# First mixer: input blocks and token projection as whole fp32 products without splits; the compression product in four groups of 32 columns

## The chip, the cores and the metric

The kernel runs on one core of one Trainium2 chip. The metric is the device time of one execution in microseconds (us). The engines: PE is TensorE (matrix products), DVE is VectorE, ACT is ScalarE, POOL is GpSimd, SP is SyncE, which only issues transfers here.

## The reference

Two layers of a causal decoder for 256 tokens of width 1024. The change lies in the first mixer of layer 0 alone: an input projection shared by a convolution branch and a sparse-attention branch. Cut to what it computes:

```python
a = val * jax.nn.sigmoid(gate)                     # 512 channels each, from the input projection
y = lax.conv_general_dilated(a, conv_w[:, None, :], ...)     # 31 taps, per channel
y = silu(layernorm(y + conv_b))

def compress_blocks(src, pos, w1, w2):             # once for keys, once for values
    blk = src[:, idx] + pos[None, None, :, None, :]          # 15 blocks of 32 tokens, stride 16
    blk = blk.transpose(0, 3, 1, 2, 4).reshape(B, NSA_KV_HEADS, n_cmp, CMP_LEN * HEAD_DIM)
    return jax.nn.gelu(blk @ w1) @ w2              # 2 heads x 15 blocks, 2048 -> 256 -> 64
...
h = h + concat(y, attention) @ w_out
```

After it come, per layer, an expert mixer (PEER) that multiplies by all 16,384 experts' keys and values, and gates; they are not changed.

## The kernel before, in words

Everything is held transposed: `h` is 128 partitions x 8 slices (kt) x 256 tokens. The PEER products run from about 170 us to the end and the change does not touch them; the function `u_dense` they share is only given a width argument.

**Splits.** A product of the mixer in full precision is made of three passes at a rounded type (fp32r). `split` (L264, L265) makes the rounded part `hnH` of the normed input on ACT and the rest `hnL` on DVE. Each weight block `wx` (128 x 1024, 512 KB, 16 blocks of `in_win`, then 8 of `in_wout`) is split in the same way: `prep_h` (L184) makes `wH` on ACT and `prep_l` (L197) makes `wL` on DVE. `u_block` then issues for each of the 8 kt three matmuls (`mm3`, L225, L226, L227), 24 for one block of 128 x 256 outputs.

**Fetches.** Blocks are fetched on SP (L166) into a ring of three buffers; a buffer is free again once `wL` is made, so DVE sets when a fetch may start.

**Order.** The table `STEPS` (L46) says in which order the pieces of the mixer are written: first four channel pairs of the convolution (8 blocks, in the loop of L474), then the steps of the table. C, K and Q are input blocks (the last, Q3, is block 15); T1 and T3 are convolution taps on PE (L442, on diagonal matrices `dg` that ACT makes, L441); W1 and W0 are the token projection `in_token` (values and gates, weights `wt` of 128 x 8 x 280, split in step S at L545 and L546); s0 to s3 are scores (L640, L642, then P on ACT at L649); M0 and M1 are `compress`; p0, p1 are scores against compressed keys (L604); w0 to w3 weigh the values (L674, L684, L692); L is one stage of the normalisation of the convolution (L713, L726). The other convolution taps run one by one on DVE (L459), three behind most steps. A scheduler then orders the instructions within each engine. The sums of squares for the norm (ACT L282, PE L306) stand behind the first block, and everything that leaves PE is scaled by the norm `rs` afterwards.

**compress(c)** (L565): 16 fp32 matmuls with 30 columns of blocks as weights and 256 columns of `w1` as moving operand, into 30 partitions (L569); Gelu on ACT into `hid` (L572, with a table load before it); two transposes (L575); a copy `hT` (L578); the product with `w2` (L584 or L587).

Of the kernel before, what the change touches and what calls it, by code (L numbers as in the profile page):

```python
# [35 lines left out]
RINGS, ROWBUFS, AHEAD = (3, 10), 7, 8  # L36
# [9 lines left out]
STEPS = ("T1 Q1 C0 C1 K0 K1 B1 Q0 Q2 T3 B0 S W1 Q3 s0 M0 s1 W0 s2 p0 M1 w0 L w1 s3 p1 w2 L w3 L"  # L46
# [9 lines left out]
class Trunk:  # L56
# [72 lines left out]
    def plan(self):  # L129
# [22 lines left out]
        self.split_range(0, at["wq", 0] + 7)  # L152
# [90 lines left out]
    def u_dense(self, k, x):  # L243

        w = self.raw_block(k)
        out = self.bank()[:, :ND]
        for kt in range(KT):
            m = self.nc.tensor.matmul(out, w[:, kt * 128:kt * 128 + 128], x[:, kt, :ND],  # L248
                                      start=kt == 0, stop=kt == KT - 1)
        self.last_mm[k] = m  # L250
        self.raw_done(k)
        return out
# [145 lines left out]
    def mixer_even(self, st):  # L398
# [3 lines left out]
        base = self.at["in"]  # L402

# [70 lines left out]
        for c in range(4):  # L474
            pv = self.u_block(base + 2 * c)
# [4 lines left out]
            pg = self.u_block(base + 2 * c + 1)  # L480
# [19 lines left out]
        def in_kc(c):  # L500

            pk = self.u_block(next(nxt))
# [6 lines left out]
            blk.append((mp.tile([128, 16, 2, 15], F32, name=f"blk{c}"), E))  # L509
# [5 lines left out]
        def in_k(c):  # L515
            pk = self.u_block(next(nxt))
            for g in range(2):
                r = slice(g * 64, g * 64 + 64)
                nc.vector.tensor_tensor(out=kz[r, g, c], in0=pk[r], in1=self.rs[r], op=ALU.mult)

        def blocks(c):
            bt, E = blk[c]
            for g in range(2):
                v = E[g][:, 1:257].rearrange("p (n r) -> p r n", r=16)
                for hf in range(2):
                    pos = cpos[:, c, hf * 8:hf * 8 + 8, None].to_broadcast([128, 8, 15])
                    nc.vector.tensor_tensor(out=bt[:, hf * 8:hf * 8 + 8, g],
# [4 lines left out]
        def in_q(c):  # L532
            pq = self.u_block(next(nxt))
# [3 lines left out]
        wtH = mp.tile([128, KT, 280], F32R, name="wtH")  # L537
        wtL = mp.tile([128, KT, 280], F32R, name="wtL")
        vt = mp.tile([128, 2, 256], F32, name="vt")
        gt = mp.tile([128, 2, 24], F32, name="gt")  # L540

        def split_wt():
            for hf in range(2):
                s = slice(hf * 4, hf * 4 + 4)
                nc.scalar.activation(wtH[:, s], wt[:, s], AF.Copy)  # L545
                nc.vector.tensor_tensor(out=wtL[:, s], in0=wt[:, s], in1=wtH[:, s].bitcast(F32),  # L546
                                        op=ALU.subtract)

        def in_token(tt):
            pv = self.bank()[:, :280]  # L550
            s = slice(tt * 128, tt * 128 + 128)
            for kt in range(KT):
                self.mm3(pv, self.hnH[:, kt, s], self.hnL[:, kt, s], wtH[:, kt], wtL[:, kt],
                         kt == 0, kt == KT - 1)
# [10 lines left out]
        def compress(c):  # L565

            ph = self.bank()
            for lp in range(16):
                nc.tensor.matmul(ph[0:30, :256], blk[c][0][:, lp].rearrange("p g n -> p (g n)"),  # L569
                                 w1[c][:, lp], start=lp == 0, stop=lp == 15)  # L570
            hid = mp.tile([30, 256], F32, name="hid", bufs=1)
            nc.scalar.activation(hid, ph[0:30, :256], AF.Gelu_apprx_tanh)  # L572
            pt = self.bank()
            for m in range(2):
                nc.tensor.transpose(pt[:, m * 32:m * 32 + 30], hid[:, m * 128:m * 128 + 128],  # L575
                                    self.ident[0:30, 0:30])
# [246 lines left out]
    def peer_and_ple(self, l, st):  # L823
# [63 lines left out]
        for i in range(NB):  # L887
# [11 lines left out]
            ps = self.u_dense(base + i, hn)  # L899
# [553 lines left out]
```

## Time and profile before

| what | us |
|---|---|
| median of 3 runs (lowest, highest) | 1529.66 (1528.58, 1530.78) |
| the profiled execution's own time | 1531.44 |
| its span, first to last instruction | 1529.7 |
| PE busy in the span | 1499.5 (98%) |
| DVE, ACT, POOL busy | 1142.0, 684.7, 446.1 |
| the mixer: first matmul to the first product with `wout` | 5.56 to 128.82 |

A busy PE is one with a matmul under way; the granted clock tells separately how fast it ran (mean 0.993 of full). In the timeline, "start us" is the time from the span's start, and a row with xN is N instructions in a row as one. The duration of a matmul contains the time in which its results drain, so what a stream of them costs is read from the distance of their starts.

### The profile page before, as it was taken

The numbers are of one execution on the slowest core, as the hardware profiler recorded it, in microseconds if no ns is written. First come the engines' busy times: TensorE is split into PE (matmuls) and PEld (weight loads), VectorE is DVE, ScalarE is ACT, GpSimd is POOL, SyncE is SP. The second block draws the span as 40 slices with busy tenths as digits, with TensorE's granted clock in tenths as the row PEclk, the third lists the DMA queues.
The fourth block names the chain that finished last, engine by engine and source line by source line (L and its number), as shares of the span: only waits on it lengthen the run. The fifth ranks groups of instructions, "written<-read, shape, count | busy, mean of one in ns | idle before, by whom it ended". The sixth has DMA issues, their size and how long they took to land.

```text
span 1529.7 us, 30252 instructions
## 1 busy us (share of the span) xinstructions
PE 1499.5 (98%) x11882; PEld 1457.0 (95%) x11882; DVE 1142.0 (75%) x2752; ACT 684.7 (45%) x864; POOL 446.1 (29%) x406
## 2 busy tenths in 40 slices
PE   8999999999999999999998999999999999999997
PEld 8858999999999999999998999999999999999997
DVE  6997699988876888544448699987886788644446
ACT  6468321358863876000036321248872877000025
POOL 0000014343444333444300004343444333343400
PEclk9999999999999999999999999999999999999998
DMA  6603679999999999999985279999999999999980
GB/s 239 231 1 113 233 238 409 408 408 408 408 396 396 402 381 378 405 409 408 409 347 166 89 231 400 408 409 408 409 388 393 409 380 367 408 408 409 409 315 28
DMA packets 141245, 514.83 MB, mean 337 GB/s; under 512 B 15984, under 2 KB 16240, under 8 KB 140592
## 3 DMA queue, kind: packets, MB, share of 16 engines
q1 hardware_dynamic: 84384, 308.42, 52.6%
q0 software_dynamic: 55568, 202.66, 33.7%
q8 instruction: 94, 1.54, 0.4%
q10 hardware_dynamic: 1152, 1.82, 0.4%
q14 instruction: 47, 0.39, 0.1%
HBM read 511.53 MB, written 1.05 MB: 335 GB/s over the span
## 4 chain that ended last, share of the span: by engine, by line
PE 76%; DMA 12%; DVE 10%; ACT 1%; issue 1%; DVEq 0%; SPq 0%; ACTq 0%
PE bank_a L1015 28%; PE bank_a L248 26%; DMA wx<-in_v 9%; PE bank_g L1246 5%; PE bank_a L225 3%; PE bank_a L226 3%; PE bank_a L227 3%; DMA wx<-in_u 3%; DVE row L1341 2%; PE bank_a L569 1%; DVE rt_tmp L1033 1%; PE bank_a L640 1%; DVE yc L459 1%; PE bank_r L306 1%; DVE wL L197 1%
## 5 line engine op out<-in xcount | busy, mean ns | idle before, releaser
L1015 PE MATMUL bank_a<-z,wx 128*128 128x160 f32 x4096 | 574.6, 301 | 3.9 <-DMA wx<-in_v 1.0
L248 PE MATMUL bank_a<-hn,wx 128*128 128x160 f32 x4096 | 569.8, 300 | 2.1 <-DVE rt_gs L1204 1.2
L1015 PEld LDWEIGHTS bank_a<-z,wx 128*128 128x128 f32 x4096 | 559.3, 190 | 11.1 <-DMA wx<-in_v 11.0
L248 PEld LDWEIGHTS bank_a<-hn,wx 128*128 128x128 f32 x4096 | 558.7, 190 | 4.9 <-issue 1.8
L1235 ACT ACTIVATE o<-sq 128x512 fp8e4<-128x512 f16 x160 | 398.6, 2599 | 46.7 <-DVE sq L1227 46.5
L1314 POOL DMA_INDIRECT row<-in_ur,sp_idx x192 | 228.2, 1188 | 475.4 <-PE bank_a L248 193.7
L1351 DVE SCALAR_TENSOR_TENSOR sp_acc<-row,sp_w,sp_acc 128x1024 f32<-128x1024 f32 x188 | 241.7, 1286 | 153.1 <-DMA row<-in_v,sp_idx 152.4
L1314 POOL DMA_INDIRECT row<-in_v,sp_idx x192 | 210.0, 1094 | 333.8 <-PE bank_a L1015 220.3
L1341 DVE SCALAR_TENSOR_TENSOR row<-row,sp_x 128x1024 f32<-128x1024 f32 x192 | 231.1, 1217 | 31.5 <-DMA row<-in_ur,sp_idx 31.5
L184 ACT ACTIVATE wH<-wx 128x1024 fp32r<-128x1024 f32 (+1 forms) x63 | 65.4, 1042 | 389.0 <-DMA wx<-in_proj 338.1
L1008 ACT ACTIVATE z<-bank_a 128x160 f32<-128x160 f32 x256 | 95.8, 379 | 285.9 <-PE bank_a L248 285.2
L1251 DVE SCALAR_TENSOR_TENSOR z<-bank_g,z 128x512 f32<-128x512 f32 x80 | 93.1, 1163 | 66.2 <-PE bank_g L1246 66.2
L197 DVE TENSOR_TENSOR wL<-wx,wH 128x1024 fp32r<-128x1024 f32 (+1 forms) x63 | 75.8, 1204 | 50.9 <-ACT wH L184 50.4
L225 PE MATMUL bank_a<-hnH,wH 128*128 128x256 f32 x320 | 93.5, 295 | 6.0 <-ACT wH L184 5.6
L227 PE MATMUL bank_a<-hnH,wL 128*128 128x256 f32 x320 | 93.0, 292 | 0.3 <-DVE wL L197 0.3
L226 PE MATMUL bank_a<-hnL,wH 128*128 128x256 f32 x320 | 92.8, 291 | 0.0
L1246 PE MATMUL bank_g<-sq,o 128*128 128x64 f16 x1280 | 89.5, 237 | 0.0
L1246 PEld LDWEIGHTS <-o 128*128 128x128 fp8e4 x1280 | 82.6, 113 | 3.0
L1231 DVE TENSOR_TENSOR sq<-o,gHL 128x512 f16<-128x512 f16 x160 | 68.0, 425 | 11.1
L225 PEld LDWEIGHTS bank_a<-hnH,wH 128*128 128x128 f32 x320 | 63.2, 199 | 7.0 <-ACT wH L184 5.8
L1227 DVE TENSOR_TENSOR sq<-iota,i2T 128x512 f16<-128x512 f16 x160 | 67.2, 420 | 0.0
L227 PEld LDWEIGHTS bank_a<-hnH,wL 128*128 128x128 f32 x320 | 63.6, 199 | 0.7 <-DVE wL L197 0.6
(313 smaller groups left out, 1208.6 us busy)
## 6 DMA issues: line engine op xcount, KB each, us to landing
wx<-in_u SPq DMA_DIRECT2D x256, 512.0 KB, 13.1
wx<-in_v SPq DMA_DIRECT2D x256, 512.0 KB, 11.6
wx<-in_wq SPq DMA_DIRECT2D x16, 512.0 KB, 3.7
wx<-in_gatew SPq DMA_DIRECT2D x16, 512.0 KB, 6.5
wx<-in_win SPq DMA_DIRECT2D x15, 512.0 KB, 6.1
w<-in_cw SPq DMA_DIRECT2D x2, 2048.0 KB, 9.9
wx<-in_wout SPq DMA_DIRECT2D x8, 512.0 KB, 3.8
row<-in_ur,sp_idx POOLq DMA_INDIRECT x192, 9.6
```

What stands on the lines that cost most here:

```text
L225: mm(out, wH, xH, start=start, stop=False, **kw)
L226: mm(out, wH, xL, start=False, stop=False, **kw)
L227: mm(out, wL, xH, start=False, stop=stop, **kw)
L248: m = self.nc.tensor.matmul(out, w[:, kt * 128:kt * 128 + 128], x[:, kt, :ND], start=kt == 0, stop=kt == KT - 1)
L1008: self.nc.scalar.activation(z[i // HB][:, i % HB], ps, AF.Gelu_apprx_tanh)
L1015: m = self.nc.tensor.matmul(acc[kt // 2][:, (kt % 2) * ND:(kt % 2) * ND + ND], w[:, kt * 128:kt * 128 + 128], x, start=b == 0 and kt % 2 == 0,
L1235: nc.scalar.activation(o8.rearrange("p t e -> p e t"), o2, AF.Copy, saturate=False)
L1246: nc.tensor.matmul(ps[k][:, c:c + HB], o8[:, t], og[:, p, :, t], start=p == 0, stop=p == 1)
L1251: nc.vector.scalar_tensor_tensor(v, ps.pop(k).rearrange("p (t b) -> p t b", b=HB), 1.0 / GSCALE, v, op0=ALU.mult, op1=ALU.mult)
L1314: ins = k.nc.gpsimd.indirect_dma_start(out=G, out_offset=None, in_=table, in_offset=bass.IndirectOffsetOnAxis(ap=self.idx[:, c:c + 1], axi ...
L1341: nc.vector.scalar_tensor_tensor(G, G, 1.0, self.x[u], op0=ALU.mult, op1=ALU.mult, accum_out=self.dot[:, col])
L1351: nc.vector.scalar_tensor_tensor(self.acc[u], G, self.w[:, col], self.acc[u], op0=ALU.mult, op1=ALU.add)
```

## The change

The hidden input is scaled by the norm's gain once, as fp32 (`hx`, eight instructions on ACT), and not split. The 16 input blocks and the token projection are products of whole fp32 operands: 8 matmuls where there were 24, and no split of `in_win` or `wt`, so a ring buffer is freed by the last matmul on it. The ring has four buffers. Splits begin with `wout`, whose first two blocks are split behind step Q3. In `compress` the blocks are padded with zeros to 32 columns and the 16 matmuls go by turns to four groups of 32 partitions; `hid` is the plain copy of all four on 128 partitions, two matmuls with a stack of four identities (`sel[1]`) sum and transpose them at once, and Gelu follows at `hT`. Lines move: L248 is the whole product, L403 `hx`, L443 and L444 the PE taps, L548 the token projection, L565, L568, L572, L575, L580 and L583 `compress`.

```diff
-RINGS, ROWBUFS, AHEAD = (3, 10), 7, 8
+RINGS, ROWBUFS, AHEAD = (4, 10), 7, 8
...
-STEPS = ("T1 Q1 C0 C1 K0 K1 B1 Q0 Q2 T3 B0 S W1 Q3 s0 M0 s1 W0 s2 p0 M1 w0 L w1 s3 p1 w2 L w3 L"
+STEPS = ("T1 Q1 C0 C1 K0 K1 B1 Q0 Q2 T3 B0 W1 Q3 s0 M0 s1 W0 s2 p0 M1 w0 L w1 s3 p1 w2 L w3 L"
...
-        self.split_range(0, at["wq", 0] + 7)
+        self.split_range(at["wout"], at["wq", 0] + 7)
...
-    def u_dense(self, k, x):
+    def u_whole(self, k, x, n):
 
         w = self.raw_block(k)
-        out = self.bank()[:, :ND]
+        out = self.bank()[:, :n]
         for kt in range(KT):
-            m = self.nc.tensor.matmul(out, w[:, kt * 128:kt * 128 + 128], x[:, kt, :ND],
+            m = self.nc.tensor.matmul(out, w[:, kt * 128:kt * 128 + 128], x[:, kt, :n],
                                       start=kt == 0, stop=kt == KT - 1)
         self.last_mm[k] = m
         self.raw_done(k)
...
         st = self.stats_open()
-        for kt in range(KT):
-            self.split(kt, self.h[:, kt], self.vecs[:, V_MIX[0], kt:kt + 1])
         st = self.mixer_even(st)
...
         base = self.at["in"]
+        hx = mp.tile([128, KT, T], F32, name="hx")
+        for kt in range(KT):
+            nc.scalar.activation(hx[:, kt], self.h[:, kt], AF.Copy,
+                                 scale=self.vecs[:, V_MIX[0], kt:kt + 1])
...
-            pv = self.u_block(base + 2 * c)
+            pv = self.u_whole(base + 2 * c, hx, T)
             if c == 0:
                 for kt in range(KT):
                     self.stats_sq(st, kt)
                     self.stats_mm(st)
-            pg = self.u_block(base + 2 * c + 1)
+            pg = self.u_whole(base + 2 * c + 1, hx, T)
...
-            pk = self.u_block(next(nxt))
+            pk = self.u_whole(next(nxt), hx, T)
...
-            blk.append((mp.tile([128, 16, 2, 15], F32, name=f"blk{c}"), E))
+            bt = mp.tile([128, 16, 32], F32, name=f"blk{c}")
+            nc.gpsimd.memset(bt[:, :, 30:32], 0.0)
+            blk.append((bt, E))
...
-            pq = self.u_block(next(nxt))
+            pq = self.u_whole(next(nxt), hx, T)
...
-        def split_wt():
-            for hf in range(2):
-                s = slice(hf * 4, hf * 4 + 4)
-                nc.scalar.activation(wtH[:, s], wt[:, s], AF.Copy)
-                nc.vector.tensor_tensor(out=wtL[:, s], in0=wt[:, s], in1=wtH[:, s].bitcast(F32),
-                                        op=ALU.subtract)
...
             for kt in range(KT):
-                self.mm3(pv, self.hnH[:, kt, s], self.hnL[:, kt, s], wtH[:, kt], wtL[:, kt],
-                         kt == 0, kt == KT - 1)
+                nc.tensor.matmul(pv, hx[:, kt, s], wt[:, kt], start=kt == 0, stop=kt == KT - 1)
...
-            ph = self.bank()
+            ph = self.bank()[:, :256]
+
             for lp in range(16):
-                nc.tensor.matmul(ph[0:30, :256], blk[c][0][:, lp].rearrange("p g n -> p (g n)"),
-                                 w1[c][:, lp], start=lp == 0, stop=lp == 15)
-            hid = mp.tile([30, 256], F32, name="hid", bufs=1)
-            nc.scalar.activation(hid, ph[0:30, :256], AF.Gelu_apprx_tanh)
-            pt = self.bank()
+                q = lp % 4 * 32
+                nc.tensor.matmul(ph[q:q + 32], blk[c][0][:, lp], w1[c][:, lp], start=lp < 4,
+                                 stop=lp >= 12, skip_group_check=True)
+            hid = mp.tile([128, 256], F32, name="hid", bufs=1)
+            nc.scalar.activation(hid, ph, AF.Copy)
+
+            pt = self.bank()[:, :64]
             for m in range(2):
-                nc.tensor.transpose(pt[:, m * 32:m * 32 + 30], hid[:, m * 128:m * 128 + 128],
-                                    self.ident[0:30, 0:30])
+                nc.tensor.matmul(pt[:, m * 32:m * 32 + 32], hid[:, m * 128:m * 128 + 128],
+                                 self.sel[1], start=True, stop=True)
             hT = mp.tile([128, 2, 32], F32, name="hT", bufs=2)
-            nc.scalar.activation(hT[:, :, 0:30],
-                                 pt[:, 0:64].rearrange("p (m n) -> p m n", m=2)[:, :, 0:30], AF.Copy)
+            nc.scalar.activation(hT.rearrange("p m n -> p (m n)"), pt, AF.Gelu_apprx_tanh)
...
+            if step == "Q3":
+                self.prep_l(self.at["wout"] + 1)
```

The queue of ACT at the start, from the first table load on. Before, `hnH` and the first splits stand first and the squares (`sq`) between them:

```order
L316 ACTIVATE warm<-eps 128x1
L264 ACTIVATE hnH<-h,vecs 128x256 x2
L184 ACTIVATE wH<-wx 128x512
L282 ACTIVATE sq<-h 128x256
L184 ACTIVATE wH<-wx 128x512
L282 ACTIVATE sq<-h 128x256
L264 ACTIVATE hnH<-h,vecs 128x256 x6
L282 ACTIVATE sq<-h 128x256 x3
```

The same queue with the change:

```order
L316 ACTIVATE warm<-eps 128x1
L282 ACTIVATE sq<-h 128x256 x8
L322 ACTIVATE rq_s<-bank_r,eps 128x2
L316 ACT_TABLE_LOAD
L316 ACTIVATE warm<-rq_s,eps 128x1
L403 ACTIVATE hx<-h,vecs 128x256 x8
L413 DMA cvec<-in_cvec 128x136
```

All eight squares, the root of their sum (`rq_s`, which reads what PE summed in `bank_r`) and a table load now stand ahead of the first `hx`, which the first product reads.

ACT around step T3, where the last taps on PE are made: before

```order
L184 ACTIVATE wH<-wx 128x1024 x4
L441 ACTIVATE dg<-ident,cvec 128x128 x2
L184 ACTIVATE wH<-wx 128x1024
L462 ACTIVATE yc_162<-yc_162,cvec 128x256
L184 ACTIVATE wH<-wx 128x1024 x2
L441 ACTIVATE dg<-ident,cvec 128x128 x4
L555 ACTIVATE vt<-bank_a,rq_r 128x256
```

and with the change, where the three `wH` are of `wout` blocks:

```order
L443 ACTIVATE dg<-ident,cvec 128x128 x5
L184 ACTIVATE wH<-wx 128x1024
L464 ACTIVATE yc_157<-yc_157,cvec 128x256
L464 ACTIVATE yc_156<-yc_156,cvec 128x256
L184 ACTIVATE wH<-wx 128x1024
L443 ACTIVATE dg<-ident,cvec 128x128 x2
L184 ACTIVATE wH<-wx 128x1024
L443 ACTIVATE dg<-ident,cvec 128x128 x4
L549 ACTIVATE vt<-bank_a,rq_r 128x256
```

The splits of input blocks are gone from the queue; the last four `dg` stand behind the third split of a `wout` block, as they stood behind the seventh `wH` of this piece before.

ACT in step M0 (`compress` for the keys): before

```order
L649 ACTIVATE P_936,sm<-bank_a,mx 128x128 x8
L462 ACTIVATE yc_163<-yc_163,cvec 128x256
L572 ACT_TABLE_LOAD
L572 ACTIVATE hid<-bank_a 30x256
L578 ACTIVATE hT<-bank_a 128x2x30
L592 ACTIVATE kcz<-bank_a 64x15 x2
L649 ACT_TABLE_LOAD
```

and with the change:

```order
L645 ACTIVATE P_589,sm<-bank_a,mx 128x128 x8
L568 ACTIVATE hid<-bank_a 128x256
L575 ACT_TABLE_LOAD
L575 ACTIVATE hT<-bank_a 128x64
L588 ACTIVATE kcz<-bank_a 64x15 x2
L464 ACTIVATE yc_158<-yc_158,cvec 128x256
L645 ACT_TABLE_LOAD
```

The load of the Gelu table has moved from ahead of `hid` to behind it, and `hid` still stands behind the eight P of step s0. PE's queue keeps the order of the steps; in M1 the fourth product of the mean (L713, L709 with the change) has moved from step w1 up behind `compress`.

## Rows read from the trace of the kernel before

**Rows 1.** The page: a costly group, split on DVE: busy us, mean ns, idle before.

```profile
L197 DVE TENSOR_TENSOR wL<-wx,wH 128x1024 fp32r<-128x1024 f32 (+1 forms) x63 | 75.8, 1204 | 50.9 <-ACT wH L184 50.4
```

**Rows 2.** PE's waits, 0 to 165 us: line, releaser, us in total, times, longest.

```profile
PE bank_a L225 <- ACT wH L184: 5.6, 1, 5.6
```

**Rows 3.** Timeline of PE: start us, us, line, operation, out<-in, count [idle before].

```profile
5.56 0.58 PE L225 MATMUL bank_a<-hnH,wH 128*128 128x256 f32 x1 [5.56 <-ACT wH L184]
...
18.01 0.41 PE L225 MATMUL bank_a<-hnH,wH 128*128 128x256 f32 x1
...
22.71 0.31 PE L225 MATMUL bank_a<-hnH,wH 128*128 128x256 f32 x1
...
23.10 0.61 PE L338 MATMUL bank_r<-sq,ones 128*128 128x128 f32 x4
...
24.26 0.28 PE L225 MATMUL bank_a<-hnH,wH 128*128 128x256 f32 x1
24.38 0.28 PE L226 MATMUL bank_a<-hnL,wH 128*128 128x256 f32 x1
...
64.10 1.03 PE L442 MATMUL bank_g<-ap,dg 128*128 128x256 f32 x4
```

**Rows 4.** Timeline of PE from the scores s0 through step M0.

```profile
73.66 1.02 PE L640 MATMUL bank_a<-kz,qT 128*128 128x512 f32 x2
...
75.89 7.09 PE L569 MATMUL bank_a<-w,blk 128*30 128x256 f32 x32
...
84.41 1.12 PE L640 MATMUL bank_a<-kz,qT 128*128 128x512 f32 x2
```

**Rows 5.** Timeline of ACT at the start.

```profile
8.66 1.71 ACT L264 ACTIVATE hnH<-h,vecs 128x256 fp32r<-128x256 f32 x4 [0.27 <-DMA h<-in_xT]
...
17.62 0.26 ACT L322 ACTIVATE rq_s<-bank_r,eps 128x2 f32<-128x2 f32 x1 [1.34 <-PE bank_r L306]
...
18.19 1.28 ACT L316 ACT_TABLE_LOAD   x1
19.48 0.29 ACT L316 ACTIVATE warm<-rq_s,eps 128x1 f32<-128x1 f32 x1
```

**Rows 6.** Timeline of PE in layer 1, after its longest wait.

```profile
841.84 0.94 PE L306 MATMUL bank_r<-ones,sq 128*128 128x1 f32 x4 [4.34 <-DVE sq L287]
...
848.76 0.30 PE L225 MATMUL bank_a<-hgH,wH 128*128 128x256 f32 x1
```

**Rows 7.** DMA issues, 0 to 165 us: KB each, median us from issue to landing.

```profile
wx<-in_win SPq DMA_DIRECT2D x15, 512.0 KB, 6.1
...
wx<-in_wout SPq DMA_DIRECT2D x8, 512.0 KB, 3.8
```

**Rows 8.** Timeline of ACT around T3.

```profile
62.00 1.06 ACT L184 ACTIVATE wH<-wx 128x1024 fp32r<-128x1024 f32 x1 [2.03 <-DMA wx<-in_wout]
```

**Rows 9.** Timeline of PE from M1 through w1.

```profile
94.55 7.09 PE L569 MATMUL bank_a<-w,blk 128*30 128x256 f32 x32
...
102.97 0.97 PE L604 MATMUL bank_r<-kcz,qT 128*128 128x30 f32 x8
...
105.04 0.61 PE L674 MATMUL bank_a<-ident,Pc 128*15 128x128 f32 x4
...
107.03 1.08 PE L692 MATMUL bank_g<-PT,vt 128*64 128x256 f32 x8
108.05 0.61 PE L674 MATMUL bank_a<-ident,Pc 128*15 128x128 f32 x4
...
112.24 1.12 PE L640 MATMUL bank_a<-kz,qT 128*128 128x512 f32 x2
```

**Rows 10.** Timeline of ACT in step M0.

```profile
78.57 0.40 ACT L649 ACTIVATE P<-bank_a,mx 128x128 f32<-128x128 f32 x1
...
81.00 1.28 ACT L572 ACT_TABLE_LOAD   x1
83.02 0.37 ACT L572 ACTIVATE hid<-bank_a 30x256 f32<-30x256 f32 x1 [0.74 <-PE bank_a L569]
```

More of the change, by code (lines that the diff above doesn't have):

```diff
@@ L515, in in_k @@
         def in_k(c):
-            pk = self.u_block(next(nxt))
+            pk = self.u_whole(next(nxt), hx, T)
             for g in range(2):
@@ L526, in blocks @@
                     pos = cpos[:, c, hf * 8:hf * 8 + 8, None].to_broadcast([128, 8, 15])
-                    nc.vector.tensor_tensor(out=bt[:, hf * 8:hf * 8 + 8, g],
+                    nc.vector.tensor_tensor(out=bt[:, hf * 8:hf * 8 + 8, g * 15:g * 15 + 15],
                                             in0=v[:, 0::2, hf:hf + 15], in1=pos, op=ALU.add)
@@ L532, in in_q @@
         def in_q(c):
-            pq = self.u_block(next(nxt))
+            pq = self.u_whole(next(nxt), hx, T)
             nc.vector.scalar_tensor_tensor(qT[c], pq, 0.125, self.rs, op0=ALU.mult, op1=ALU.mult)
-        wtH = mp.tile([128, KT, 280], F32R, name="wtH")
-        wtL = mp.tile([128, KT, 280], F32R, name="wtL")
         vt = mp.tile([128, 2, 256], F32, name="vt")
         gt = mp.tile([128, 2, 24], F32, name="gt")
-        def split_wt():
-            for hf in range(2):
-                s = slice(hf * 4, hf * 4 + 4)
-                nc.scalar.activation(wtH[:, s], wt[:, s], AF.Copy)
-                nc.vector.tensor_tensor(out=wtL[:, s], in0=wt[:, s], in1=wtH[:, s].bitcast(F32),
-                                        op=ALU.subtract)
         def in_token(tt):
@@ L744, in mixer_even @@
         ln = conv_norm()
-        steps = {"T": pe_taps, "C": in_kc, "K": in_k, "Q": in_q, "B": blocks, "S": split_wt,
+        steps = {"T": pe_taps, "C": in_kc, "K": in_k, "Q": in_q, "B": blocks,
                  "W": in_token, "M": compress, "p": compressed, "s": scores, "w": weigh}
@@ L898, in peer_and_ple @@
             step(self.GATE_NS if i > HB else self.DENSE_NS if sparse.ready else self.ROUTE_NS)
-            ps = self.u_dense(base + i, hn)
+            ps = self.u_whole(base + i, hn, ND)
             if pend is not None:
```

## The prediction

> **What bounds the kernel now.** I read first the costliest groups of the mixer, then what PE waited for, then PE's timeline stage by stage. The groups show DVE loaded with splits, 1.20 us for a block [rows 1], so taking them away looks like a gain. The waits say otherwise: in the first 165 us PE waits long only once, 5.6 us for the first split block [rows 2]. After that it is fed. The timeline has the blocks 0 and 1 done at 23.10, and blocks 2 to 14 run until 64.10 [rows 3]. So here PE's own stream sets the time; work removed from DVE and ACT is worth nothing except where PE waits for them, which is at the start and around each `compress`. Two prices follow. A split matmul of 256 columns takes 0.120 at the full clock (24.26 to 24.38) and 0.2136 at the half level (22 starts from 18.01 to 22.71) [rows 3]: the granted clock is at one of its two levels, 2.4 and 1.2 GHz, and the same matmul shows which. A whole fp32 matmul is two passes; 32 of them take 7.09, the last draining for about 0.4, so a pass is 0.216 [rows 4].
>
> **The change part by part.** Differences to before in us, plus is slower.
>
> *A. The start.* Before, PE begins at 5.56 [rows 3], between the squares. Now the last quarter of `h` lands at 8.66, and four squares at no more than the 0.43 that `hnH` took each end at about 10.4 [rows 5]. PE sums them in about 1.3 (four small passes of this kind are 0.94 at the half clock [rows 6]): 11.7. The root takes 0.26, the load of the next table 1.28, and its first `hx` about 0.4 [rows 5], with a warm-up of 0.3: PE starts block 0 near 14.1, 8.5 later. Against that stand two blocks at 16 matmuls of 0.43 (full) or 0.86 (half) instead of 48 split ones plus sums. If the clock rises near 19.3, 6 matmuls run at half and 10 at full: 5.2 + 4.3, done at 23.6 against 23.10: **+0.5**. The rise can come as late as 20.9, since after the longest pause of layer 1 PE ran 6.9 at half, 841.84 to 848.76 [rows 6], which gives 24.4 (+1.3); or the clock is full at once, which gives 21.0 (-2.1).
>
> *B. Blocks 2 to 14.* One block was 24 x 0.120 = 2.88 and is 16 passes x 0.216 = 3.46: +0.58 for each, 13 times +7.5. Before, the 13 blocks and the 6 taps of T1 (12 passes) should take 37.4 + 2.6 = 40.0; from 23.46, where the sums of the norm end, to 64.10 they took 40.6. I give the 0.6 back, since the splits that caused it are gone: **+6.9**. The bounds are 6.5 and 8 (a late fetch). The ring is now freed by PE: a buffer is freed one block's end and needed three blocks, 10.4, later, against a median landing of 6.1 for `in_win` [rows 7]; this covers it, and a transfer that takes over 10.4 costs what it takes beyond.
>
> *C. T3, W1, Q3.* Before, 64.10 to 73.66 is 9.56 [rows 3, 4]: taps 16 x 0.216 = 3.46, W1 24 x 0.131 (0.120 by columns) = 3.15, Q3 2.88. After: taps the same, W1 16 x 0.236 = 3.78, Q3 3.46, together 10.7. One stall is new: the last four `dg` on ACT stand behind the third split of `wout`. Counted from the end of block 12, which frees the buffer: landing 3.8 [rows 7], `wH` 1.06 [rows 8], `wL` 1.20 [rows 1], landing 3.8, `wH` 1.06, then `dg`, 0.4: 11.3. PE gets to the fifth tap after two blocks, four taps and four products of W1, 6.9 + 1.7 + 1.9 = 10.5. A stall of 0.8 and a little for the pace of `dg`: 1.0 (between 0 and 2.5). **+2.1**. So the scores begin about 9.5 later than before.
>
> *D. M0.* From s0's start to s1's start was 84.41 - 73.66 = 10.75 [rows 4], of which `compress` took 7.1. The bounds of the four groups are the serial 6.9 and a quarter, 1.73. The nearest row is L692, where matmuls of 64 columns go to two groups: 8 passes are over in 1.08, not in 8 x 0.216 = 1.73 and a drain [rows 9]; so two groups run side by side, and I take four, 1.9 with filling. The product ends 2.2 + 1.9 = 4.1 after s0's start, but `hid` stands behind the eight P, whose last ended at 78.97, 5.3 after s0's start [rows 10]; with an emptier DVE I take 4.9. So `compress` is hidden up to 2.7. Then `hid` 0.4 [rows 10], and the load, which was hidden before (81.00, two us ahead of `hid` [rows 10]), is on the path: 1.28; `hT` 0.25, L580 0.35: 7.2. **-3.5**, between -3.0 and -3.8.
>
> On the load, the trace has the next activation right behind the 1.28 (18.19 to 19.48 [rows 5]). The Trainium skill ("ScalarE: Activation LUTs", the step on the table-load gate) puts a switch at about 2.7 with its drain, and by it M0 and M1 would each give back 1.4; the trace speaks against it.
>
> *E. W0.* 3.78 for 3.15: **+0.6**.
>
> *F. M1.* From the start of `compress` to w0 was 105.04 - 94.55 = 10.5 [rows 9]. After: 1.9, four products of the mean 8 x 0.216 = 1.73, L600 0.81 are 4.4 on PE; beside them `hid`, the load and `hT` on ACT end at about 5.4 (ACT first finishes s2's P and two short steps), then the product with `w2` 0.55: 6.0. **-4.5**, between -3.4 (the chain on ACT a us longer) and -4.9.
>
> *G. The tail.* w0 took 3.01, w1 4.19, 108.05 to 112.24 [rows 9]. The difference is a product of the mean, now in M1, and waits for it and for the last taps on DVE, which end earlier now: **-1.2**, between -0.6 and -2. The `wout` product that follows keeps its order and its splits, and so does all that comes after: 0.
>
> The sum is 0.5 + 6.9 + 2.1 - 3.5 + 0.6 - 4.5 - 1.2 = **+0.9**. Made against the profiled execution, whose span is 1529.7 and own time 1531.44, that is a span of 1530.6. The median of the runs is 1.8 under the profiled execution's own time; the difference goes onto the median: 1529.66 + 0.9 = **1530.6**. A measurement of this kernel can tell about 0.2%, 3.06 us, from no change, and the runs before spread over 2.2. So the forecast is: no difference.
>
> **The rivals.**
>
> *Four groups do not overlap as four* (slower). The two passes of one fp32 matmul are on the same group, and if PE starts passes strictly in the order of the program, a second pass holds up the next group's first: two side by side, 16 x 0.216 = 3.5. M0 then ends its product at 5.7, 0.8 to 1.0 beyond the P, and M1 adds 1.6 in PE's queue: +2.6, **1533.2**. It decides as soon as the product takes over 2.7. For it: L692 shows two at a time, never more. Against: the two there start together, in pairs of the same time, which a strict order by passes would not give. If nothing overlaps, 6.9: +9, 1539.6; L692 speaks against it.
>
> For packing the Trainium skill ("TensorE: Matmul & The Clock Gate", Part 3, on measured speedups) has three column groups at 2.38 times and says that matmuls start and end strictly in program order; four groups at three quarters of the ideal, an estimate from it, would be 2.3, still hidden in M0.
>
> *The clock falls in M0* (slower). PE is nearly idle between the end of the product (4.1) and s1 (7.2), some 3 us; before, it was busy there with the product. After the 4.34 wait of layer 1 the clock was at the half level [rows 6]. If it falls here, the scores and W0 behind it run at half for 3.4 to 6.9, which costs half of that: +1.7 to +3.4, **1533.1** in the middle. Against it: the pause is shorter than 4.3 and not quite empty.
>
> *A longer chain at T3*: landings of 5 instead of 3.8 make C +2.4 worse: 1533.0.
>
> *Faster*: the clock is full at the first block (-2.6 against A), no stall at T3 (-1.0) and the tail gives 2 (-0.8): **1526.2**. For it: PE is not quite idle before 14.1. Against: before, the clock needed until 22.7 to stay up [rows 3].
>
> *The change does not do what it says*: the whole products could be stalled by late `hx` or fetches; the order shows `hx` complete ahead of the products, so only fetches are left, which is inside B.
>
> **How the numbers follow.** Forecast 0.45; the pairs 0.13 and no overlap 0.05; the clock in M0 0.15; T3 0.05; faster 0.17. Faster by over 0.2%: the faster rival, 0.17. Slower by over 0.2%: no overlap, the pairs (3.5 over before), half of the clock and of T3, little of the forecast: 0.30. Within: 0.53. The range goes from 1526.2, the faster rival, to 1534.4, which takes in the pairs, T3 and the upper part of the clock and leaves out no overlap. The forecast's own range is 1528.5 to 1532.5.
>
> **What would show it.** PE's first block at about 14, after `hx`; blocks at 3.46 and nothing waiting between; the scores at about 83; L565 x32 in about 2 us, and s1 7.2 after s0; w0 6 after M1's start; the first product with `wout` within 2 us of 128.82. A block stream with waits for transfers, an L565 of over 2.7, half-level spacing after M0, or a difference behind 170 us would prove a step wrong.

## The result, and the profile after

The changed kernel takes **1538.76 us** (median of 6 runs, 1535.84 to 1540.2) against 1529.12 for the kernel before in the same comparison (1525.73 to 1530.95): a ratio of **1.0061, 95% interval 1.0045 to 1.0077**. It is slower by 9.6 us, outside the range that was given. The profiled execution has a span of 1536.7 and an own time of 1538.54.

PE's timeline with the change (start us, us, line, operation, count [idle before]):

```profile
7.13 5.28 PE L306 MATMUL bank_r<-ones,sq 128*128 128x1 f32 x24 [0.83 <-ACT sq L282]
14.77 10.05 PE L248 MATMUL bank_a<-hx,wx 128*128 128x256 f32 x32 [2.36 <-ACT hx L403]
24.65 0.61 PE L338 MATMUL bank_r<-sq,ones 128*128 128x128 f32 x4
...
48.34 0.70 PE L444 MATMUL bank_g<-ap,dg 128*128 128x256 f32 x2 [0.63 <-ACT dg L443]
...
50.18 23.47 PE L248 MATMUL bank_a<-hx,wx 128*128 128x256 f32 x108
73.49 1.03 PE L444 MATMUL bank_g<-ap,dg 128*128 128x256 f32 x4
74.35 1.11 PE L548 MATMUL bank_a<-wt,hx 128*128 128x280 f32 x4
77.64 1.13 PE L444 MATMUL bank_g<-ap,dg 128*128 128x256 f32 x4 [2.19 <-ACT dg L443]
78.61 2.03 PE L548 MATMUL bank_a<-wt,hx 128*128 128x280 f32 x4
80.43 1.83 PE L444 MATMUL bank_g<-ap,dg 128*128 128x256 f32 x4
...
88.31 1.02 PE L636 MATMUL bank_a<-kz,qT 128*128 128x512 f32 x2
...
90.55 1.94 PE L565 MATMUL bank_a<-w,blk 128*32 128x256 f32 x32
93.92 0.63 PE L572 MATMUL bank_a<-sel,hid 128*128 128x32 f32 x4 [1.43 <-ACT hid L568]
95.45 0.44 PE L580 MATMUL bank_a<-hT,w 128*64 128x15 f32 x8 [0.90 <-ACT hT L575]
95.83 2.08 PE L636 MATMUL bank_a<-kz,qT 128*128 128x512 f32 x2
...
103.47 1.02 PE L636 MATMUL bank_a<-kz,qT 128*128 128x512 f32 x2
...
108.25 1.93 PE L565 MATMUL bank_a<-w,blk 128*32 128x256 f32 x32
...
114.23 0.61 PE L670 MATMUL bank_a<-ident,Pc 128*15 128x128 f32 x4
```

Its first product with `wout` (L225) starts at 136.76, where the kernel before has 128.82: +7.94. From there to the end the span differs by -0.9. So all of the loss lies in the stretch that the prediction took apart, and can be read against it stage by stage. Each difference is that of the stage's first and last start in these rows and in [rows 3, 4, 9]; s2 started at 89.77 before.

| stage | before | after | difference | predicted |
|---|---|---|---|---|
| A, to the end of blocks 0 and 1 | 23.10 | 24.65 | +1.55 | +0.5 |
| B, to the first tap of T3 | 41.00 | 48.84 | +7.84 | +6.9 |
| C, T3, W1, Q3 | 9.56 | 14.82 | **+5.26** | +2.1 |
| D, s0 to s1 | 10.75 | 7.52 | -3.23 | -3.5 |
| E, s1 and W0 | 5.36 | 7.64 | **+2.28** | +0.6 |
| s2, p0 | 4.78 | 4.78 | 0 | 0 |
| F, M1 to w0 | 10.49 | 5.98 | -4.51 | -4.5 |
| G, the tail | 23.78 | 22.53 | -1.25 | -1.2 |

The packed product did what it was to do: 32 passes in 1.94, where they took 7.09 [rows 4]. What failed is in front of it and behind it. A view of two stretches shows the clock (the stretch, its us, then busy time of PE, PEld, DVE, ACT, POOL, the granted clock, DMA share, GB/s):

```profile
79.00:81.00 2.00, 2.00 (x6) 1.49 (x5) 1.23 (x1) 1.21 (x3) 0.00 (x0) 0.50 0.73 215
...
97.00:99.00 2.00, 2.00 (x5) 0.70 (x3) 0.64 (x1) 1.61 (x2) 0.00 (x0) 0.50 0.00 0
```

Behind PE's pause of 2.19 in T3 and behind the pause in M0 (1.43 and 0.90, with a short product between) the granted clock is 0.50, that is 1.2 GHz. From 78.61 to 82.11 PE does 3.50 us of work that takes 1.8 by the rows at full clock beside it; s1 takes 3.87 (95.83 to 99.70) instead of 2.14 before. That is 1.7 us each time.

DVE's timeline tells why T3 waited:

```profile
73.68 1.22 DVE L197 TENSOR_TENSOR wL<-wx,wH 128x1024 fp32r<-128x1024 f32 x1
74.81 1.00 DVE L461 SCALAR_TENSOR_TENSOR yc<-ap,cvec,yc 128x256 f32<-128x256 f32 x2
75.73 0.42 DVE L538 SCALAR_TENSOR_TENSOR qT<-bank_a,rs 128x256 f32<-128x256 f32 x1
77.33 1.23 DVE L197 TENSOR_TENSOR wL<-wx,wH 128x1024 fp32r<-128x1024 f32 x1 [1.19 <-ACT wH L184]
79.66 1.23 DVE L197 TENSOR_TENSOR wL<-wx,wH 128x1024 fp32r<-128x1024 f32 x1 [1.10 <-ACT wH L184]
83.64 0.48 DVE L458 SCALAR_TENSOR_TENSOR yc<-ap,cvec,bank_g 128x256 f32<-128x256 f32 x1 [2.76 <-PE bank_g L444]
```

and ACT's:

```profile
75.84 0.51 ACT L464 ACTIVATE yc<-yc,cvec 128x256 f32<-128x256 f32 x1 [1.54 <-DVE yc L461]
76.26 1.04 ACT L184 ACTIVATE wH<-wx 128x1024 fp32r<-128x1024 f32 x1
77.21 0.68 ACT L443 ACTIVATE dg<-ident,cvec 128x128 f32<-128x128 f32 x2
78.57 1.06 ACT L184 ACTIVATE wH<-wx 128x1024 fp32r<-128x1024 f32 x1 [0.68 <-DMA wx<-in_wout]
```

The chain goes round all three engines. The first `wL` of `wout` stands on DVE (73.68) in front of two last taps (74.81); a bias step on ACT (L464 at 75.84) waits 1.54 for them; the next `wH` and the `dg` stand behind it on ACT; PE waits for `dg`; and DVE's first tap of channel 3 waits for PE's T3 (83.64). DVE is not full here: from 70 to 84 it idles 5.05 (1.19, 1.10 and 2.76 in the rows), waiting for `wH` and for T3. The 23 taps of channel 3 then stand before and between the score maxima. In this execution that does no harm: the first maximum (L642) starts at 89.97, 1.66 after the scores, and did so 1.79 after them before. It does harm where the scores come earlier (e3).

### The profile page after: what moved, and what is told of

The parts are those of the page before. It is cut to its first block, busy times and chain, and to the rows that moved or that the text cites. A ratio compares the mean times of both kernels' runs of the same rounds, so it can differ in the third digit from the quotient of the medians.

```text
span 1536.7 us, 29902 instructions
## 1 busy us (share of the span) xinstructions
PE 1502.8 (98%) x11742; PEld 1456.0 (95%) x11742; DVE 1122.7 (73%) x2725; ACT 665.9 (43%) x844; POOL 451.3 (29%) x408
## 4 chain that ended last, share of the span: by engine, by line
PE 72%; DMA 13%; DVE 13%; ACT 1%; issue 1%; SPq 0%; DVEq 0%; ACTq 0%
PE bank_a L1013 29%; PE bank_a L248 24%; DMA wx<-in_v 8%; DMA wx<-in_u 5%; PE bank_g L1244 5%; DVE yc L461 3%; PE bank_a L225 3%; PE bank_a L227 3%; PE bank_a L226 3%; DVE row L1339 2%; DVE rt_tmp L1031 1%; PE bank_a L636 1%; PE bank_r L306 1%; DVE rt_ixd L1035 0%; PE bank_r L1360 0%
## 5 line engine op out<-in xcount | busy, mean ns | idle before, releaser
L248 PE MATMUL bank_a<-hn,wx 128*128 128x160 f32 x4096 | 572.3, 301 | 2.9 <-DVE rt_gs L1202 1.2
L248 PEld LDWEIGHTS bank_a<-hn,wx 128*128 128x128 f32 x4096 | 559.1, 190 | 8.0 <-issue 4.5
L1312 POOL DMA_INDIRECT row<-in_v,sp_idx x192 | 213.8, 1114 | 330.5 <-PE bank_a L1013 203.8
L184 ACT ACTIVATE wH<-wx 128x1024 fp32r<-128x1024 f32 x46 | 48.5, 1056 | 388.7 <-DMA wx<-in_proj 336.0
L197 DVE TENSOR_TENSOR wL<-wx,wH 128x1024 fp32r<-128x1024 f32 x46 | 56.2, 1223 | 44.7 <-ACT wH L184 43.9
L248 PE MATMUL bank_a<-hx,wx 128*128 128x256 f32 x256 | 59.2, 393 | 2.4 <-ACT hx L403 2.4
L248 PEld LDWEIGHTS bank_a<-hx,wx 128*128 128x128 f32 x256 | 50.6, 198 | 9.8 <-ACT hx L403 2.4
L225 PE MATMUL bank_a<-hnH,wH 128*128 128x256 f32 x192 | 54.0, 286 | 0.5 <-ACT hnH L695 0.5
L226 PE MATMUL bank_a<-hnL,wH 128*128 128x256 f32 x192 | 54.2, 284 | 0.0
L227 PE MATMUL bank_a<-hnH,wL 128*128 128x256 f32 x192 | 54.2, 283 | 0.0
```

Of the source, the lines that this page charges most:

```text
L225: mm(out, wH, xH, start=start, stop=False, **kw)
L226: mm(out, wH, xL, start=False, stop=False, **kw)
L227: mm(out, wL, xH, start=False, stop=stop, **kw)
L1312: ins = k.nc.gpsimd.indirect_dma_start(out=G, out_offset=None, in_=table, in_offset=bass.IndirectOffsetOnAxis(ap=self.idx[:, c:c + 1], axi ...
```

## The experiments

Each ratio is to runs of the kernel before that were taken beside it (11 to 32 of them, medians 1528.83 to 1529.81), so rows are compared by their ratios.

| run | us, median | ratio to before, 95% | first `wout` product |
|---|---|---|---|
| compress alone (e1) | 1541.36 | 1.0075 (1.0055 to 1.0096) | 131.18 |
| whole products alone (e2) | 1545.68 | 1.0099 (1.0082 to 1.0115) | 145.12 |
| more `dg` (e3) | 1537.44 | 1.0042 (1.0026 to 1.0057) | 136.67 |
| W0 in M0 (e4) | 1540.94 | 1.0084 (1.0062 to 1.0106) | 139.97 |
| e3, `wL` on POOL (e5) | 1539.80 | 1.0073 (1.0050 to 1.0097) | 136.57 |
| `hx` on POOL (e6) | 1537.36 | 1.0064 (1.0040 to 1.0088) | 135.67 |
| e1, half of `wL` on POOL (e7) | 1543.74 | 1.0083 (1.0059 to 1.0108) | 141.18 |
| before, half of `wL` on POOL (e8) | 1545.45 | 1.0103 (1.0076 to 1.0129) | 144.80 |
| T3 early (e9) | 1538.21 | 1.0055 (1.0035 to 1.0075) | 136.11 |
| `hx` early (e10) | 1530.73 | 1.0016 (1.0002 to 1.0030) | 132.93 |
| `hx`, T3 early (e11) | 1534.98 | 1.0036 (1.0021 to 1.0052) | 133.46 |
| the same, W0 in M0 (e12) | 1534.50 | 1.0026 (1.0008 to 1.0044) | 128.00 |
| split held (e13) | 1535.67 | 1.0042 (1.0028 to 1.0056) | 133.74 |
| `hx` early, split held (e14) | 1528.51 | **0.9997** (0.9982 to 1.0012) | 128.24 |
| the same, T3 early (e15) | 1528.95 | 0.9995 (0.9984 to 1.0007) | 128.10 |
| the same, W0 in M0 (e16) | 1534.65 | 1.0035 (1.0021 to 1.0048) | 134.17 |
| e14 with s0 in M0 (e17) | 1528.29 | 0.9992 (0.9981 to 1.0004) | 126.46 |
| e15 with s0 in M0 (e18) | 1528.55 | 0.9997 (0.9987 to 1.0008) | 127.57 |

The last column is from the profiled execution. From there to the end of its own time the profiled executions take 1398.0 (e15) to 1404.6 (e13), so a shift of 3 us or less is judged by the ratios, not by one trace.

**The two parts alone.** e1 puts only `compress` of the change into the kernel before:

```diff
-                nc.tensor.matmul(ph[0:30, :256], blk[c][0][:, lp].rearrange("p g n -> p (g n)"),
-                                 w1[c][:, lp], start=lp == 0, stop=lp == 15)
+                q = lp % 4 * 32
+                nc.tensor.matmul(ph[q:q + 32], blk[c][0][:, lp], w1[c][:, lp], start=lp < 4,
+                                 stop=lp >= 12, skip_group_check=True)
...
```

> The kernel before with the new compression product alone: blocks padded to 32 columns, four groups, Gelu behind the sum; all split products stay. Theory 1 (the parts add up): M0 gives 3.2, M1 4.5, and a pause of PE in M0 costs about 1.7 of half clock: 1529.1 - 6.0 = 1523. Theory 2 (the split work on DVE holds the gain back): in the kernel before the last convolution tap on DVE ends at 107.9 with DVE busy without a gap from 35 on, so PE that is 7 us earlier must wait for the mean's products; the gain is 0 to 3, 1526 to 1529.

e2 is the changed kernel with the same lines turned back.

> The changed kernel with the old compression product: only the whole products are new. Theory 1: start +1.6, blocks 2 to 14 +7.7, T3 to Q3 +5.3, W0 +0.6, together +15.2 against before, less what the tail gains (about 1): 1543. Theory 2 (much of the loss comes from the pause in M0 that the new compression makes): no half clock behind M0 here, and the time is under 1541.

e2 came out near theory 1. e1 was a surprise: **slower** than before, although the product is as short as in the change (L573 x32 in 1.93). Some of its waits:

```profile
PE bank_a L678 <- DVE Pc L626: 2.6, 1, 2.6
PE bank_r L717 <- ACT yc L462: 1.6, 1, 1.6
PE bank_a L580 <- ACT hid L576: 1.6, 1, 1.6
PE bank_r L730 <- ACT ap L724: 1.5, 1, 1.5
```

With split products DVE is full (10.00 of 10 from 70 to 90, as it is before), so an earlier PE only waits for it, and the clock falls behind the waits (0.80 to 0.86 over each 10 us from 90 to 130). From w0 to `wout` this execution takes 36.18, where the kernel before takes 23.78. It is the fastest of its six (1534.22). Their mean granted clock is 0.984 to 0.990, that of the runs of before beside them 0.992 to 0.995; the means differ by 0.0065, an estimate of 10 us, so most of the 0.75% is time at half level, but where the slower executions spend it was not profiled. The parts are not additive (0.75 and 0.99% alone, 0.61% together). That the whole products free the DVE time which the packed one needs fits this, but is not tested by itself.

**T3's pause.** e3 gives each of the 14 `dg` a buffer of its own:

```diff
-                dg = mp.tile([128, 128], F32, name="dg", bufs=2)
+                dg = mp.tile([128, 128], F32, name="dg", bufs=14)
```

> The changed kernel with 14 buffers for the diagonal matrices of the PE taps instead of 2, so that ACT makes all of them at the start and nothing of T1 and T3 waits behind ACT's later queue. Theory 1 (PE's waits for these matrices, 0.6 in T1 and 2.2 in T3, and the half clock that follows the second, about 1.7): -4.5, to 1534.3, with no half clock between 70 and 90 us. Theory 2 (the wait moves to the next late thing, such as a fetched block): less than 1.5 of gain.

The wait in T3 is gone and the scores start at 84.02, 4.3 earlier, but in this execution the end stays (`wout` at 136.67): the taps and the three `wL` are as late as before, the first score maximum on DVE comes 5.06 after the scores, and M0 waits for `hid` behind it.

```profile
89.08 0.69 DVE L642 TENSOR_REDUCE mx<-bank_a 128x4 f32<-128x512 f32 x1
...
93.03 1.06 PE L572 MATMUL bank_a<-sel,hid 128*128 128x32 f32 x4 [4.84 <-ACT hid L568]
```

e9 moves T3 up instead:

```diff
-STEPS = ("T1 Q1 C0 C1 K0 K1 B1 Q0 Q2 T3 B0 W1 Q3 s0 M0 s1 W0 s2 p0 M1 w0 L w1 s3 p1 w2 L w3 L"
+STEPS = ("T1 T3 Q1 C0 C1 K0 K1 B1 Q0 Q2 B0 W1 Q3 s0 M0 s1 W0 s2 p0 M1 w0 L w1 s3 p1 w2 L w3 L"
```

> The change, with one entry of the order table moved: the PE taps of channel block 3 (T3) stand right behind those of block 1 instead of behind Q2. Theory 1 (the pause in front of T3 in the changed kernel is set by work on ACT that waits for the conv taps on DVE, and it costs its 2.2 us and then some 1.7 us of half clock; the taps of channel 3 also start late for the same reason): no wait for dg and no half level between 75 and 85 us, channel 3's taps start before 70 us instead of 83.6, the score maxima are not held up, the first w_out product comes at 131 to 134 us (136.76 in the changed kernel) and the median is 1533 to 1536. Theory 2 (DVE is what is full, and moving T3 moves the wait to M0 as with the larger dg buffer): M0's wait for hid grows to 3 us or more with half clock behind it, w_out at 136 or later, median 1537 to 1540.

Theory 2: a wait of 4.32 for `hid`, half clock behind it, `wout` 0.65 earlier, the ratio not told apart from the change's. So the pause in T3 was one place where the late `wL` and taps came out, not their cause.

**Filling M0, and POOL.** e4 writes W0 into M0, behind the copy `hid`:

```diff
             nc.scalar.activation(hid, ph, AF.Copy)
+            if c == 0:
+                in_token(0)
...
```

> The changed kernel with the token projection W0 written inside M0, between the compression product and the sum of its groups, so that PE has 3.8 us of work while ACT finishes the probabilities, the copy, the table load and the Gelu. Theory 1 (the pause in M0 costs its idle 2.3 and then about 1.7 of half clock): -4, to 1534.8, and no half clock between 92 and 105. Theory 2 (the pause alone counts, the clock falls anyway): -2.3, to 1536.5. Theory 3 (the scores s1 and what stands behind come late enough on ACT and DVE that the pause comes back later): less than 1.

Theory 3: `hT` then waits on ACT behind other work, 2.6 and 1.9 us, and the clock is at half from 115 to 121.

POOL was tried as relief for DVE, with the three `wL` of `wout` (e5, on top of e3) and, as a control, with every second `wL` of `in_win` in both e1 (e7) and the kernel before (e8). The lines are those of e7 and e8:

```diff
-                nc.vector.tensor_tensor(out=L[:, q], in0=x[:, q], op=ALU.subtract,
-                                        in1=self.hl[k][0][:, q].bitcast(F32))
+                eng = nc.gpsimd if k < 16 and k % 2 else nc.vector
+                eng.tensor_tensor(out=L[:, q], in0=x[:, q], op=ALU.subtract,
+                                  in1=self.hl[k][0][:, q].bitcast(F32))
```

> The kernel with 14 diagonal buffers (run e3), and the splits wL of the first three output blocks moved from DVE to POOL. In e3 PE came to M0 4.3 us earlier and waited 4.8 there: the maxima of the scores stood on DVE behind the taps of channel 3, and these behind two wL of output blocks that waited for their transfers, DVE idle 1.2 and 1.3 ahead of them. Theory 1 (DVE's queue behind those splits is what holds M0): the taps of channel 3 start at about 77 instead of 81.2, M0's pause falls from 5.3 to under 2, and the time from 1537.4 to about 1533. Theory 2 (23 taps at 0.5 each are too many behind T3 wherever they start, or the transfers themselves hold ACT): less than 1.5 of gain.

> The kernel before with every second wL of the input blocks on POOL, nothing else: the control for e7. Both theories of the study say that PE's own stream bounds the kernel before, so that DVE's relief alone gives nothing: within 1.5 of 1529.8. If DVE did bound it, the time falls by 2 or more; if POOL is too slow for a split, it rises.

It makes things worse, in e8 by 1.03%. What DVE does at the same time gets slower. The groups of DVE from 20 to 110 us, e8 (busy, mean ns):

```profile
L460 DVE SCALAR_TENSOR_TENSOR yc<-ap,cvec,yc 128x256 f32<-128x256 f32 x100 | 52.9, 573 | 0.7 <-ACT yc L455 0.3
```

and the same group of the kernel before:

```profile
L459 DVE SCALAR_TENSOR_TENSOR yc<-ap,cvec,yc 128x256 f32<-128x256 f32 x106 | 47.1, 475 | 0.2
```

e5 shows it at one place: nine taps take 8.60 while POOL makes two `wL` in 4.91, and M0 waits 5.8 for `hid`. POOL itself is slow too: in e8 a `wL` takes it 2.36 to 3.80, DVE 1.22, and PE waits 3.0 for those of POOL, 4.1 for those of DVE and 5.1 for `dg`. How the 1.03% divides between the two is not shown. e7 was to tell whether DVE alone holds back the gain of e1 (1523 if so). It is slower than before (1.0083), with the same waits for POOL and `dg` in it, and tells nothing on `compress`.

**The start.** e6 makes `hx` on POOL.

> The changed kernel with the eight scaled inputs hx made on POOL instead of ACT, where they stood behind the root and its table load. Theory 1 (ACT's order holds the first product back): PE starts block 0 behind its sums, at about 12.4 instead of 14.8, and the clock rises earlier by as much: -2.4, to 1536. Theory 2 (the clock's rise follows the products and the norm holds what comes next, or POOL is slow): less than 1 of gain.

Theory 2: PE's first block still begins at 14.83, and the two are done at 25.15. What holds `hx` is not ACT. POOL waits with it for DVE:

```profile
13.80 7.31 POOL L403 TENSOR_SCALAR hx<-h,vecs 128x256 f32<-128x256 f32 x8 [11.56 <-DVE ident L101]
```

`hx` lies where a set-up tile (`jp`) lay that DVE reads to make `ident` (L101). In the changed kernel this stands on DVE behind `rq_v`, a step of the norm:

```profile
12.74 0.16 DVE L325 TENSOR_SCALAR rq_v<-bank_r 128x2 f32<-128x2 f32 x1 [11.70 <-ACT rq_s L322]
12.82 0.22 DVE L101 TENSOR_SCALAR ident<-jp 128x128 f32<-128x128 int32 x1
```

e10 keeps that tile elsewhere, and nothing else:

```diff
-        with self.pool("tmp") as tmp:
-            jp = tmp.tile([128, 128], I32, name="jp")
+        jp = per.tile([128, 128], I32, name="jp")
...
```

> The change, with the small index tile of the set-up kept in the persistent pool instead of a pool that is released, so that hx no longer lies on memory that is read by an instruction behind the statistics: hx is then scaled before or between the squares, and the first block's products run between the sums. Theory 1 (the start of the first block is held by hx, and the hold reaches the end of the stretch): the blocks 0 and 1 are done at 18 to 20 us (24.65 in the changed kernel), half level until then, and the median is 3 to 5 us under the changed kernel's, 1533.5 to 1536. Theory 2 (DVE, full from 30 us on, takes it back): the first w_out product stays within 1.5 us of 136.76, with PE's waits for dg and hid longer by what the start gave; median 1537 to 1539.

```profile
5.25 2.04 PE L247 MATMUL bank_a<-hx,wx 128*128 128x256 f32 x4 [5.25 <-DMA wx<-in_win]
...
20.43 0.61 PE L337 MATMUL bank_r<-sq,ones 128*128 128x128 f32 x4
...
73.42 1.13 PE L443 MATMUL bank_g<-ap,dg 128*128 128x256 f32 x4 [2.19 <-ACT dg L442]
```

PE starts at 5.25, blocks 0 and 1 are done 4.2 earlier (20.43), and the ratio falls from 1.0061 to 1.0016, beyond what theory 1 expected. The 4.2 is no chance of one execution: in the eight profiled runs with `hx` early the two blocks are done at 19.09 to 21.87, in the eight others of the changed kernel's start at 23.32 to 25.73. The wait in T3 is the same 2.19, but in this execution the clock stays full behind it and is at half behind M0 instead, from 90 to 96.6. The rest of the gain, beyond the 3.8 that `wout` comes earlier in the trace, lies in executions that were not profiled: the twelve fall into five of 1533.71 to 1536.11, the profiled one (1534.93) among them, and seven of 1529.29 to 1531.46, whose mean granted clock is higher (0.994 to 0.997 against 0.992 to 0.994).

> Both of the two edits before: the index tile in the persistent pool and T3 right behind T1. Theory 1 (both holds are separate, and with T3 out of the way DVE has its work spread): first w_out product at 126 to 129 us, median 1528 to 1532, that is level with or just under the kernel before. Theory 2 (with the start earlier DVE is the bound through the blocks and only one of the gains is left): w_out at 131 to 134, median 1533 to 1536, with a wait of 3 us or more for hid or for mx in front of M0's second part.

> Both of the two edits before, and W0 issued inside M0 between the four groups' product and the fold, so that PE has work while ACT makes hid. Theory 1 (M0's pause of 1.4 us and the half clock behind it, 1.7 us, are then hidden, and nothing new waits): 1.5 to 3 us under the run with the two edits, 1525 to 1529. Theory 2 (as when W0 was moved alone: hT waits for ACT behind the exponentials, and half clock comes later instead): within 1 us of the run with the two edits, or up to 2 us later.

e11: theory 2 again, 4.33 for `hid`. e12's profiled execution has no half clock up to `wout` and takes 1529.89, but its 12 runs reach from 1526.64 to 1539.23: a fill that leaves `hT` waiting 1.8 us does not hold.

**The split of `wout`.** The change places it behind Q3. e13 holds its first three `wH` back until M0's `hT` (and with them the `wL`):

```diff
+        self.tc.add_manual_dep(m.ins, self.hold.ins.name, mybir.DependencyInfo(
+            mybir.DependencyClass.Sync, mybir.DependencyReason.DATA), reason="behind hT")
...
-            if step == "Q3":
+            if step == "M0":
                 self.prep_l(self.at["wout"] + 1)
```

> The change alone, but the split of the first three w_out blocks (three wH on ACT, three wL on DVE), which the change puts behind the last block of the stretch, is held until M0's hT is made. Theory 1 (DVE is the engine that is late behind the blocks, and the 3.7 us of wL with their waits stand in front of the taps and of the score maxima): the wait for dg in front of T3 falls from 2.2 to under 1.3 us, DVE doesn't idle between 76 and 84, the scores start at 85.5 to 87.5 (88.31 in the changed kernel), w_out at 133 to 135.5 (136.76), median 1534.5 to 1537. Theory 2 (the taps alone set it, the split filled holes): w_out within 1 us of 136.76, median 1537.5 to 1540.

```profile
75.70 1.13 PE L450 MATMUL bank_g<-ap,dg 128*128 128x256 f32 x4 [0.60 <-ACT dg L449]
...
85.15 1.02 PE L644 MATMUL bank_a<-kz,qT 128*128 128x512 f32 x2
...
90.86 0.63 PE L578 MATMUL bank_a<-sel,hid 128*128 128x32 f32 x4 [1.53 <-ACT hid L574]
```

Theory 1 in most of its numbers: T3 waits 0.60 and no half clock follows, the scores start 3.2 earlier, and M0's pause hardly grows (1.53 for 1.43), so the gain reaches `wout` (133.74, 3.0 earlier). One point missed: DVE still idles from 75 to 79, waiting for T3. The ratio alone does not prove the gain: 1.0042 is that of e3 too, and its interval overlaps the change's.

> The index tile in the persistent pool (hx early) and the split of the first three w_out blocks held until M0's hT. Theory 1 (the two are separate losses): 1 to 3 us under the run with hx early alone, 1527.5 to 1530, w_out at 129.5 to 132. Theory 2 (no loss from the split once the start is earlier): within 1 us of the run with hx early alone, 1530 to 1532.

> hx early, T3 right behind T1, and the split of the first three w_out blocks held until M0's hT. Theory 1 (in the run with the first two, M0 waited 4.3 us for hid because the score maxima stood behind taps and wL on DVE; the wL are 3.7 us of that): the wait for hid falls to 1.5 us or less, w_out at 128 to 131, median 1529 to 1532. Theory 2 (the taps alone hold the maxima): the wait stays over 3 us, half level behind it, median 1534 to 1536.

> hx early, T3 right behind T1, W0 inside M0, and the split of the first three w_out blocks held until M0's hT. Theory 1 (every pause of the stretch above 1 us then is one that the change made, and each has its cause named): no half level between 20 and 140 us, w_out at 125 to 127.5, median 1525 to 1529, level with or under the kernel before. Theory 2 (the waits for hT, 1.8 us each in the run without the held split, set off the half clock in most executions, whatever the start gave): median 1532 to 1535, spread over 8 us or more.

```profile
71.17 1.13 PE L449 MATMUL bank_g<-ap,dg 128*128 128x256 f32 x4 [0.60 <-ACT dg L448]
...
80.62 1.02 PE L643 MATMUL bank_a<-kz,qT 128*128 128x512 f32 x2
...
86.33 0.63 PE L577 MATMUL bank_a<-sel,hid 128*128 128x32 f32 x4 [1.54 <-ACT hid L573]
```

These rows are of e14, which settles the case: with both edits the loss is gone (0.9997, its interval well clear of the change's). The start is worth 0.45% by the ratios (1.0061 to 1.0016), clear of the intervals too. The split is 0.19% by the ratios, both in e13 (1.0061 to 1.0042) and from e10 to e14 (1.0016 to 0.9997); each of these two steps lies within the intervals, but with T3 early the same edit gives 0.41% (e11 to e15), which does not. In the traces stage C takes 11.55 in e13 and in e14, where the change takes 14.82. Of the 8.5 that e14's `wout` comes earlier than the change's, 4.4 are the start, 3.3 stage C, and 1.6 the clock behind M0, which stays full in this execution although PE pauses there as before (1.54 and 0.90). e15 agrees (theory 1, though M0 waits 2.09). e16 is theory 2 in its time: with W0 in M0 `hT` waits 1.91 and 2.51, and the half clock follows both.

**s0 inside M0.** What is left of the pause is `hid` behind the eight P on ACT. e17 and e18 put the two halves of s0 between product, fold and `hT`, which then go first on ACT:

```diff
+            if c == 0:
+                scores(0, fold)
+            else:
+                fold()
...
```

> hx early, the w_out split held until hT, and the scores s0 issued inside M0: the product of four groups, the first half of s0, the fold, the second half of s0, then hT's product; so hid and hT stand on ACT ahead of the exponentials of s0. Theory 1 (M0's pause of 1.5 and 0.9 us, which in some executions sets off the half clock behind it, is the last loss of the change that is left): no wait over 0.5 us in M0, w_out at 125 to 127, all executions without the half level there, median 1525 to 1528, under the kernel before. Theory 2 (the exponentials come 3 us later, hold the score banks, and PE waits for those instead): a wait of 1.5 us or more for a bank of s1, w_out at 127.5 to 130, median 1528 to 1533.

> The same with T3 right behind T1, so that the taps of channel 3 are done before the score maxima. Theory 1: as in the run beside it, w_out at 124.5 to 126.5, median 1524 to 1527. Theory 2: a wait of 1.5 us or more for a bank of s1, median 1528 to 1533.

M0 has no wait now, and in e17 `wout` starts at 126.46, 2.4 before the kernel before. But the first bank of s1 waits 1.53 (1.98 in e18) for the late P, and the ratio, 0.9992, reaches 1.0004: no version was shown to beat the kernel before. The runs of e17 lie within 4.1 us, those of e14 within 8.4.

## Why the prediction was wrong

- **C is the step that failed**: +5.26 for +2.1. I priced the stall by the transfers that the third `wH` waits for. That `wH` (78.57) waits 0.68 for its transfer, and PE does not wait behind it. PE waits earlier, for the `dg` behind the second `wH`, because of the taps on DVE with a `wL` ahead of them: 2.19 for my 1.0. The half clock behind the wait, 1.7, was not in the sum at all. e13 shows both gone when the split is held.
- **What bounds the kernel** was the wrong premise under it: "work removed from DVE and ACT is worth nothing except where PE waits for them". I read the places from the waits of before. In the changed kernel DVE has less to do there (7.65, 6.92 and 7.27 of 10 from 70 to 100, before 10.00 in each), and PE waits all the same, for the order in DVE's and ACT's queues. e1 shows the other side: with DVE full as before, a PE that is earlier waits. That the slow `compress` let DVE catch up before is argued from this, not shown.
- **The clock in M0**, a rival at 0.15 and +1.7 to +3.4, came true in the profiled execution: 1.7 in E, whose own +0.6 was right (2.28 together).
- **A** was +1.55 for +0.5: PE began at 14.77, not 14.1, and its starts came at the distance of the full clock only from 20.48 on, late in the bounds. More was missed in the reason: I took `hx` behind the sums as the order of the work; it was an overlap in memory, and e10 shows what the start was worth. The base, 23.10, was one execution's: e1, whose start is that of before, is done at 19.35, with the clock full from 16 to 22 where before it was at half.
- **B** was +7.84 for +6.9, the pass 0.216 as predicted. The 0.6 that I gave back did not come: the `dg` wait of 0.63 at 48.34 was not foreseen.
- **Right**: D, F and G within 0.3; four groups run as four (1.94 for 1.9), so that rival falls; the table load cost 1.28; behind `wout` the span differs by 0.9 only.
- The profiled execution of before lies 2.3 above the median of its comparison, the one of after 0.2 below its own; carrying the difference of one execution over to the medians added 2.5 to the miss. In the profiled stretch the sum was short by 7.0: C 3.2, E 1.7, A 1.0, B 0.9, D 0.3.

Take the 4.4 and the 3.3 of e14 off the +7.94 and 0.2 is left, level with before, and so is e14 by its ratio. So the trade of whole against split products and of the packed `compress` was read about rightly; what it did to DVE's and ACT's queues was not.

## What to carry to other kernels

When PE is made faster or slower at one place, ask which engines follow it one step behind, and what their queues have in front of what PE needs next; a wait removed at one place (e3, e9) comes back at the next if such an engine is late. Work that an edit places "where there is room" (here a split behind the last block) goes in front of the critical chain if the scheduler finds it ready: hold it by a dependency. A tile that reuses the memory of a released one inherits the last reader's place in its queue.

## What was not expected of the hardware

- Four column groups run side by side in full: 32 passes of one row in 1.94, against 7.09 for one group [rows 4].
- A pause of PE of about 2 us can be followed by some 3 us at half clock, and need not: behind the same 2.19 before `dg` the granted clock was 0.50 in the changed kernel and 1.00 in e10.
- Elementwise work on POOL slows DVE beside it: taps of 475 ns on average take 573 in e8, and about 960 at one place in e5 (8.60 for nine).
